# New bookings in a planner: the durations by which a hybrid encoder kernel orders its instructions, and the number of passes of its search

## The chip, the cores and the metric

The kernel runs on one core of one Trainium2 chip. TensorE (PE) does the matmuls and transposes, VectorE (DVE) and ScalarE (ACT) the elementwise work, GpSimd (POOL) a few short operations on columns, and SyncE (SP) issues nearly all DMA transfers. The metric is the device time of one execution in microseconds (us); lower is better.

## The reference, cut to what matters

Two requests of 512 tokens, width 1024, go through the same two layers in fp32: a differential-attention layer and a bidirectional retention layer. Each layer is

```
h = rms_norm(x, norm_g[i]);  q, k, v, gate = split(h @ w_in)
layer 0: p = softmax(rot(q) rot(k)^T);  o = (p[even head] - lam * p[odd head]) @ v      # 8 pairs of heads
layer 1: o = retention forward + retention backward, in chunks, with decay per head      # 8 heads
x = x + (rms_norm(o) * subln_g * silu(gate)) @ w_out
```

and a last rms_norm closes the trunk.

## The kernel before, in words

**Precision.** The matmuls take fp32r operands. Each factor is split into a rounded part (`hi_of`, a cast on ACT, L419) and the rest (`lo_of`, a subtraction on DVE, L422), and three products of the parts are summed (`PASSES`).

**Projections.** h @ w_in is done by a scheme of seven products instead of eight for blocks of two by two. The blocks of h and their sums and differences (B11, B21, T1, T2, B22, T3, T4) are made once in each layer by `make_b`: the PE transposes x into a PSUM bank (L1098), and DVE and ACT scale it by the norm's gains. A combination is one DVE instruction (`scaled`, L484: bank times gain minus another block), with further splits (L419, L422). A `Unit` is a column block of w_in; `prep` (L587, L419, L422) makes the sums of its weight blocks, and `product` the seven products P1 to P7 of a unit. A unit of kind "pair" needs 12 matmuls of 512 columns a product (`pair`, L637); a "wide" one has four steps a product of 12 matmuls of 256 columns (`wide`, L647). The sums of banks are L690 (ACT copy) and L698 (DVE), and `done` goes on from there: rotation for q and k, a silu gate (`gate_done`, L792 to L795), storing v. All of it goes out to DRAM.

**Heads.** Layer 0: scores (`scores`, L1202, 3 matmuls for each of two heads), row maxima and exponentials, a combination, a transpose (L1247), and p @ v (L1267). Layer 1: `score2` (L1400), chunk states (`state2`, L1424), products with the chunk and the far state (L1444, L1452), and norm columns (L874, L878). The output product is taken head by head (`out_step`, six matmuls of 512 columns, L950), and DVE adds it to x (L955). The last steps form the final norm and store y.

**The order.** No engine's order is written out by hand. Every operation is recorded in a list by `plan.op` with its engine, a cost in us, what it reads and writes, and, for transfers, their size. `act`, `dve`, `axpy`, `pool` and `evac` book costs that are linear in the number of elements of a partition (`dve`: 0.07 + 0.00104 n, `axpy`: 0.13 + 0.00104 n, `act`: 0.1 + 0.00083 n); `pe` gets its cost as a number. At the end, `issue` calls `arrange` several times. One call plays the whole list through on five engines (PE, ACT, DVE, POOL, SP) with the booked costs. An operation is ready once all that it depends on is done, with fixed extra times between engines (`AFTER`, `SAME`). Transfers share a bus of 380 KB a us. Whenever an engine is free it takes

- on the PE: the ready operation that is first in the program's order, at most 24 places ahead of the first one not done (`WINDOW`);
- elsewhere: the ready operation with the earliest due time (`late`). Due times are worked out backwards from the starts of the PE operations that were found in the pass before, less the costs between;
- on SP: a load only when its due time is less than 15 us away (`AHEAD`).

The first pass takes as starts the plain sum of the PE costs; each further one takes those that the pass before gave. The order of the pass with the shortest span by this count is issued. It is then fixed: each engine runs its instructions in that order and waits by semaphores. Buffers are rings (`Buf`), whose places are taken in the order of the program, and this also restricts what may be moved.

Of the kernel before, what the change touches and what calls it, by code (L numbers as in the profile page):

```python
# [16 lines left out]
S = 512  # L17
# [51 lines left out]
class Plan:  # L69
# [161 lines left out]
                    known(s)  # L231
        return out, begin, max(free.values())

    def issue(self, rounds=3):
        starts, now = {}, 0.0
        for n, op in enumerate(self.ops):
            if "PE" in op[0]:
                starts[n] = now
                now += op[0]["PE"]
        best = None  # L240
        for _ in range(rounds):
            out, begin, span = self.arrange(starts)
            if best is None or span < best[1]:
                best = (out, span, begin)
            starts = {n: begin[n] for n in starts}
        self.best = best
        for n, e in best[0]:
            costs, fn = self.ops[n][:2]
            if len(costs) > 1:
                fn(e)  # L250
            else:
                fn()
# [3 lines left out]
def trunk_kernel(  # L256
# [133 lines left out]
    def dve(n, fn, r, w, wait=0.0):  # L390
        plan.op("DVE", 0.07 + 0.00104 * n, fn, r, w, wait=wait)
# [77 lines left out]
    def make_b(layer, source):  # L469


        def parts(name, k, hi, lo, r):
            t = slot(B_SLOT[name] + k, [P, 2, S])
            hi(lambda: t[:, 0, :], r, [(t, 0)])
            lo(lambda: t[:, 1, :], lambda: t[:, 0, :], r + [(t, 0)], [(t, 1)])
            Bop[name, k] = t

        def split(name, k, src, key):
            parts(name, k, lambda out, r, w: hi_of(S, out, src, r, w),
                  lambda out, hi, r, w: lo_of(S, out, src, hi, r, w), [key])  # L480

        def scaled(out, ps, scale, less, r, w):

            dve(S, lambda: nc.vector.scalar_tensor_tensor(  # L484
                out(), ps.t, scale(), less(), op0=ALU.mult, op1=ALU.subtract), [ps, gcol] + r, w)

        def split_bank(name, k, ps, scale):
            parts(name, k, lambda out, r, w: plan.op(
                "ACT", 0.1 + 0.00092 * S,
                lambda: nc.scalar.activation(out(), ps.t, AF.Copy, scale=scale()), r + [gcol], w),  # L490
                lambda out, hi, r, w: scaled(out, ps, scale, lambda: hi().bitcast(F32), r[1:], w), [ps])

        def copy(out, ps, scale, late=()):
            evac(S, out[0], lambda: ps.t, scale, [ps, gcol, *late], [out[1]])

        def sub(out, a, b):

            dve(S, lambda: nc.vector.tensor_tensor(out[0](), a[0](), b[0](), op=ALU.subtract),
                [a[1], b[1]], [out[1]])

        def half(t, i):
            return (lambda: t[:, i, :]), (t, i)

        def whole(t):
            return (lambda: t.t), t

        two = [os_t(F32, "h") for _ in range(3)]
        h11 = [half(two[k // 2], k % 2) for k in range(4)]
        h21 = [whole(m_t("h")) for _ in range(4)]
        for name, h, k0 in (("B11", h11, 0), ("B21", h21, 4)):  # L510
            for k in range(4):
                if (name, k) in Bop and layer == 0:
                    for n in range(2):
                        ps, src = turned[n][k // 2], slice(k % 2 * 256, k % 2 * 256 + 256)
                        here = slice(n * 256, n * 256 + 256)
                        evac(256, lambda h=h[k][0], here=here: h()[:, here], lambda ps=ps, src=src: ps[:, src],
                             lambda k=k: gain(0, k), [ps, gcol, (Bop[name, k], (1, n))], [h[k][1]])
                    yield
                    continue
                bank_ = source(0, k0 + k)  # L520
                if layer == 0:
                    split_bank(name, k, *bank_)
                copy(h[k], *bank_, [(Bop[name, k], 1)] if layer == 0 else [])
                if not (layer == 0):
                    split(name, k, *h[k])
                yield
        t = [whole(e_t("h")), whole(e_t("h")), half(two[2], 0), half(two[2], 1)]
        for k in range(4):
            ps, scale = source(1, k)
            scaled(t[k][0], ps, scale, h11[k][0], [h11[k][1]], [t[k][1]])  # L530
            split("T1", k, *t[k])
            yield
        for k in range(4):
            ps, scale = source(1, 4 + k)
            scaled(t[k][0], ps, scale, t[k][0], [t[k][1]], [t[k][1]])
            split_bank("B22", k, ps, scale)
            split("T2", k, *t[k])
            sub(h11[k], t[k], h11[k])
            split("T3", k, *h11[k])
            yield  # L540
        for k in range(4):
            sub(h21[k], h21[k], t[k])
            split("T4", k, *h21[k])
            yield


    class Unit:
# [76 lines left out]
        def product(self, op, part=None):  # L624
# [27 lines left out]
            if not self.wide:  # L652
                ps = self.banks[which][0]
                if op == "P1" and self in first_units[:2]:
                    def piece(k, half):
                        here = slice(half * 256, half * 256 + 256)
                        for i, (u, v) in enumerate(PASSES):
                            nc.tensor.matmul(
                                ps[:, here], a[u][0]()[:, k, :], bt[k][:, v, here], start=(half + k + i == 0),
                                stop=(k == 3 and i == 2), skip_group_check=True)  # L660
                    if self is first_units[1]:
                        for k in range(4):
                            pe(0.7, lambda k=k: pair(ps, (k,)), reads[:2] + [bt[k]], [(ps, k)])
                        return
                    for half in range(2):
                        for k in range(4):
                            pe(0.36, lambda k=k, half=half: piece(k, half),
                               ([(a[0][1][0], (n, k // 2)) for n in range(2)] if self is first_units[0] else reads[:2])
                               + [(bt[k], (0, half)), (bt[k], (1, half))], [(ps, (k, half))])
                elif part is not None:  # L670
                    ks = range(2 * part, 2 * part + 2)
                    pe(1.4, lambda: pair(ps, ks), reads[:2] + [bt[k] for k in ks], [ps])
                else:
                    pe(2.79, lambda: pair(ps), reads, [ps])
                return
            for t in range(NT):
                ps = self.banks[which][t // 2]
                led = self.led and op == "P1" and t == 0
                pe(1.87 if led else 1.43, lambda ps=ps, t=t: wide(ps, t), reads + [ident] * led, [ps])

        def evac(self, op):
            n = 2 if self.wide else 1
# [103 lines left out]
    def gate_done(dst, gc):  # L786

        def done(i, g, tiles, s, psum):
            x = tiles[0]
            th = m_t("th") if psum else s[("c1", "c2")[g] if i == 0 else "c5"][0]  # L790
            out = th if psum else x
            act(S, lambda: nc.scalar.activation(th.t, x.t, AF.Tanh, scale=0.5), [x], [th])  # L792
            dve(S, lambda: nc.vector.scalar_tensor_tensor(out.t, th.t, 1.0, x.t, op0=ALU.add, op1=ALU.mult),
                [th, x], [out])
            act(S, lambda: nc.scalar.activation(out.t, out.t, AF.Copy, scale=gcol[:, gc + i:gc + i + 1]),  # L795
                [out, gcol], [out])
            dma(lambda: dst[g][:, i, :], lambda: out.t, [out], [(dst[g], i)], 256)
        return done
# [131 lines left out]
    def out_step(w, h, g, t, i, o, rr, last, parts=1):  # L930
# [9 lines left out]
        for p in range(parts):  # L940
# [5 lines left out]
            def fn(here=here, ps=ps):  # L946
                m = 0
                for e in range(2):
                    for a, b in PASSES:
                        nc.tensor.matmul(ps[:, here], o[a][:, e, t * P:(t + 1) * P], u[b][:, e, here],  # L950
                                         start=(m == 0), stop=(m == 5))
                        m += 1
            pe(1.39 / parts, fn, [(o[0], t // 2), (o[1], t // 2), *u], [ps])
            half = x[:, i * S + p * n:i * S + (p + 1) * n]
            axpy(n, lambda half=half, here=here, ps=ps: nc.vector.scalar_tensor_tensor(  # L955
                half, ps[:, here], rr[:, t % 2:t % 2 + 1], half, op0=ALU.mult, op1=ALU.add),
# [236 lines left out]
    def scores(i):  # L1193
        h, g, t = tiles[i]
        st[i]['s'] = []
        for j in range(2):
            s = bank("sc")
            q, k = qk[h, g, j, 0], qk[h, g, j, 1]

            def fn(s=s, q=q, k=k):  # L1200
                for n, (a, b) in enumerate(PASSES):
                    nc.tensor.matmul(s.t, q[:, a, t * P:(t + 1) * P], k[:, b, :], start=(n == 0), stop=(n == 2))  # L1202
            pe(0.7, fn, [q, k], [s])
            st[i]['s'].append(s)

    def row_max(i):
# [184 lines left out]
    def score2(b, c):  # L1391
# [5 lines left out]
        def fn():  # L1397
            for j in range(2):
                for i, (u, v) in enumerate(PASSES):
# [1 line left out]
                        s[:, j * 256:(j + 1) * 256], k[:, u, (2 * c + j) * P:(2 * c + j + 1) * P],  # L1401
                        q[:, v, c * 256:(c + 1) * 256], start=(j == 0 and i == 0), stop=(i == 2),
                        skip_group_check=True)
        pe(0.71, fn, [q, k], [s])
        t1 = e_t("rt")
        F = Fs[h]
        dve(S, lambda: nc.vector.tensor_tensor(
# [211 lines left out]
```

## Time and profile before

| | us |
|---|---|
| median of 3 runs | 1801.41 |
| lowest and highest | 1800.41, 1801.71 |
| the profiled execution | 1800.16 |
| its span, first to last instruction | 1798.3 |

The granted clock of TensorE was 0.999 of full speed. The program has 27855 instructions and moves 328.81 MB by DMA. A line in a group's row is a line of the kernel; `arena` holds the split blocks and most operands of the heads, `ws` the split weights, `raw` and `st` weights and their sums, `pj`, `sc`, `o` and `tp` are PSUM banks. In rows of the timeline, the brackets tell how long the engine was idle before the instruction and what ended it. Matmuls are pipelined: their durations overlap, and the time that one takes up is read from the spacing, as the chain of waits has it.

### The profile page before, as it was taken

The page shows a single profiled execution, that of the slowest core. Times are in us where ns is not written, and L with a number is a line of the kernel's source. Part 1 is how long each engine was busy: PE and PEld are TensorE (multiplying, and loading weights), DVE is VectorE, ACT ScalarE, POOL GpSimd, SP SyncE. Part 2 cuts the span into 40 slices and gives each one's busy share as a digit, 9 for nine tenths or more (in the row PEclk, how much of TensorE's full clock was granted, in tenths as well). Part 3 has the DMA queues.
Part 4 walks back from the last instruction along what each step waited for, and adds up shares of the span by engine and source line. Part 5 has one row for each costly group of instructions (what it writes and reads, how often), then busy time and mean ns, then how long its engine had stood idle before and what let it go on. Part 6 is the DMA issues. An engine that isn't in the chain of part 4 may idle for free.

```text
span 1798.3 us, 27855 instructions
## 1 busy us (share of the span) xinstructions
PE 1785.4 (99%) x10321; PEld 1562.1 (87%) x10321; DVE 1478.8 (82%) x2341; ACT 895.6 (50%) x1864; POOL 169.4 (9%) x315
## 2 busy tenths in 40 slices
PE   9999999999999999999999999999999999999998
PEld 7889889898988888888888888898989988888887
DVE  8967878778699888888888897777887967888887
ACT  8754344443344565455455866444434455444446
POOL 1000000000000022322232200000000000111113
PEclk9999999999999999999999999999999999999999
DMA  6444555654545695444454524465646459664652
GB/s 219 135 140 130 161 153 161 199 164 153 177 123 184 204 345 196 165 171 161 167 205 141 199 70 142 152 200 164 214 145 227 141 188 403 262 236 176 231 214 94
DMA packets 162767, 328.81 MB, mean 183 GB/s; under 512 B 12724, under 2 KB 76872, under 8 KB 162632
## 3 DMA queue, kind: packets, MB, share of 16 engines
q1 hardware_dynamic: 162304, 326.71, 53.4%
q8 instruction: 81, 1.33, 0.3%
q14 instruction: 54, 0.44, 0.1%
q10 hardware_dynamic: 328, 0.34, 0.1%
HBM read 209.55 MB, written 117.44 MB: 182 GB/s over the span
## 4 chain that ended last, share of the span: by engine, by line
PE 93%; DVE 3%; ACT 1%; DMA 1%; issue 0%; POOL 0%; SPq 0%; POOLq 0%; DVEq 0%; ACTq 0%
PE pj L637 20%; PE pj L950 19%; PE sc L637 10%; PE pj L647 10%; PE o L637 8%; PE o L1267 5%; PE sc L1202 5%; PE sc L647 5%; PE o L647 2%; PE o L1444 2%; PE tp L1247 2%; PE sc L1400 1%; PE o L1452 1%; PE tp L1424 1%; DMA raw<-in_ret_w_out_dram 1%; DVE ws L422 1%
## 5 line engine op out<-in xcount | busy, mean ns | idle before, releaser
L950 PE MATMUL pj<-ws,arena 128*128 128x512 f32 x1542 | 389.5, 396 | 0.0
L950 PEld LDWEIGHTS pj<-ws,arena 128*128 128x128 f32 x1542 | 277.5, 188 | 50.9
L637 PE MATMUL pj<-b,ws 128*128 128x512 f32 x1080 | 263.2, 390 | 0.0
L637 PEld LDWEIGHTS pj<-b,ws 128*128 128x128 f32 x1080 | 201.3, 188 | 41.3
L955 DVE SCALAR_TENSOR_TENSOR b<-pj,pad,b 128x512 f32<-128x512 f32 (+1 forms) x257 | 190.2, 744 | 23.0 <-PE pj L950 21.7
L422 DVE TENSOR_TENSOR ws<-st,ws 128x512 fp32r<-128x512 f32 (+1 forms) x192 | 148.0, 774 | 71.3 <-ACT ws L419 53.0
L422 DVE TENSOR_TENSOR ws<-raw,ws 128x512 fp32r<-128x512 f32 (+2 forms) x165 | 141.7, 863 | 68.7 <-ACT ws L419 59.1
L419 ACT CAST ws<-st 128x512 fp32r<-128x512 f32 (+1 forms) x192 | 132.2, 693 | 121.2 <-PE pj L637 36.8
L637 PE MATMUL sc<-arena,ws 128*128 128x512 f32 x768 | 185.2, 389 | 0.0
L637 PE MATMUL o<-arena,ws 128*128 128x512 f32 x744 | 178.4, 391 | 1.1 <-DVE arena L484 1.1
L637 PEld LDWEIGHTS sc<-arena,ws 128*128 128x128 f32 x768 | 143.9, 188 | 29.8
L419 ACT CAST ws<-raw 128x512 fp32r<-128x512 f32 (+2 forms) x165 | 126.0, 769 | 85.3 <-PE o L637 45.5
L637 PEld LDWEIGHTS o<-arena,ws 128*128 128x128 f32 x744 | 138.5, 188 | 30.3 <-DVE arena L484 2.0
L637 PE MATMUL pj<-arena,ws 128*128 128x512 f32 x636 | 156.1, 390 | 0.0
L637 PEld LDWEIGHTS pj<-arena,ws 128*128 128x128 f32 x636 | 118.6, 188 | 24.3
L1220 ACT ACTIVATE b<-sc,pad 128x512 f32<-128x512 f32 x128 | 87.9, 689 | 66.3 <-DVE pad L1210 64.7
L690 ACT COPY c<-pj 128x512 f32<-128x512 f32 x104 | 61.0, 587 | 116.1 <-PE pj L637 62.7
L647 PE MATMUL pj<-ws,b 128*128 128x256 f32 x960 | 116.9, 275 | 0.0
L647 PEld LDWEIGHTS pj<-ws,b 128*128 128x128 f32 x960 | 113.3, 188 | 0.6
L1202 PE MATMUL sc<-arena 128*128 128x512 f32 x384 | 100.7, 394 | 0.0
L1267 PEld LDWEIGHTS o<-arena 128*128 128x128 f32 x768 | 93.2, 188 | 2.7
L1267 PE MATMUL o<-arena 128*128 128x256 f32 x768 | 93.7, 277 | 0.0
(223 smaller groups left out, 2870.9 us busy)
## 6 DMA issues: line engine op xcount, KB each, us to landing
qk<-os SPq DMA_DIRECT2D x192, 256.0 KB, 3.5
arena<-qk SPq DMA_DIRECT2D x96, 512.0 KB, 5.7
raw<-in_da_w_in_dram SPq DMA_DIRECT2D x64, 512.0 KB, 4.9
v<-os SPq DMA_DIRECT2D x64, 512.0 KB, 3.8
arena<-v SPq DMA_DIRECT2D x64, 512.0 KB, 4.1
raw<-in_ret_w_in_dram SPq DMA_DIRECT2D x48, 512.0 KB, 4.4
os<-g SPq DMA_DIRECT2D x32, 512.0 KB, 7.8
g<-e SPq DMA_DIRECT2D x48, 256.0 KB, 4.8
```

The lines of the kernel that those rows point to most:

```text
L419: act(n, lambda: nc.scalar.copy(dst(), src()), r, w)
L422: dve(n, lambda: nc.vector.tensor_tensor(dst(), src(), hi().bitcast(F32), op=ALU.subtract), r, w)
L637: nc.tensor.matmul(ps.t, a[u][0]()[:, k, :], bt[k][:, v, :], start=(opens and k == 0 and i == 0), stop=(k == 3 and i == 2), skip_group_che ...
L647: nc.tensor.matmul(ps[:, (t % 2) * 256:(t % 2) * 256 + 256], bt[k][:, v, t * P:(t + 1) * P], a[u][0]()[:, k, :], start=(opens and t % 2 == ...
L690: act(S, lambda c=c, ps=ps: nc.scalar.copy(c.t, ps.t), [ps], [c])
L950: nc.tensor.matmul(ps[:, here], o[a][:, e, t * P:(t + 1) * P], u[b][:, e, here], start=(m == 0), stop=(m == 5))
L955: axpy(n, lambda half=half, here=here, ps=ps: nc.vector.scalar_tensor_tensor(half, ps[:, here], rr[:, t % 2:t % 2 + 1], half, op0=ALU.mult ...
L1202: nc.tensor.matmul(s.t, q[:, a, t * P:(t + 1) * P], k[:, b, :], start=(n == 0), stop=(n == 2))
L1220: act(840, lambda j=j, s=s, m=m: nc.scalar.activation(p[:, j, :], s.t, AF.Exp, bias=m.t, accum_out=sm[:, 2 * j + n:2 * j + n + 1]), [s, m] ...
L1247: nc.tensor.transpose(tp[:, j * P:(j + 1) * P], p[:, 0, j * P:(j + 1) * P], ident.t)
L1267: nc.tensor.matmul(o[:, e * 256:(e + 1) * 256], v[b][:, j, e * P:(e + 1) * P], aT[a][:, j, :], start=(n == 0), stop=(n % 12 == 11), skip_g ...
L1444: nc.tensor.matmul(o[:, e * 256:(e + 1) * 256], v_[v][:, 2 * c + j, e * P:(e + 1) * P], a_[:, u, j * 256:(j + 1) * 256], start=(e == 0 and ...
```

## The change

What changes is the number of passes (three to eight), eight booked costs of PE operations, and two bookings of elementwise work. `scaled` is recorded by `axpy` instead of `dve`, which issues the same instruction and books 0.06 us more. The last step of a gate on ACT is booked with 120 elements more. No instruction, buffer, transfer or dependence changes; only the order within each engine's queue can.

```diff
@@ -231,7 +231,7 @@
                     known(s)
         return out, begin, max(free.values())
 
-    def issue(self, rounds=3):
+    def issue(self, rounds=8):
         starts, now = {}, 0.0
         for n, op in enumerate(self.ops):
             if "PE" in op[0]:
@@ -481,7 +481,7 @@
 
         def scaled(out, ps, scale, less, r, w):
 
-            dve(S, lambda: nc.vector.scalar_tensor_tensor(
+            axpy(S, lambda: nc.vector.scalar_tensor_tensor(
                 out(), ps.t, scale(), less(), op0=ALU.mult, op1=ALU.subtract), [ps, gcol] + r, w)
 
         def split_bank(name, k, ps, scale):
@@ -660,7 +660,7 @@
                                 stop=(k == 3 and i == 2), skip_group_check=True)
                     if self is first_units[1]:
                         for k in range(4):
-                            pe(0.7, lambda k=k: pair(ps, (k,)), reads[:2] + [bt[k]], [(ps, k)])
+                            pe(0.681, lambda k=k: pair(ps, (k,)), reads[:2] + [bt[k]], [(ps, k)])
                         return
                     for half in range(2):
                         for k in range(4):
@@ -669,14 +669,14 @@
                                + [(bt[k], (0, half)), (bt[k], (1, half))], [(ps, (k, half))])
                 elif part is not None:
                     ks = range(2 * part, 2 * part + 2)
-                    pe(1.4, lambda: pair(ps, ks), reads[:2] + [bt[k] for k in ks], [ps])
+                    pe(1.362, lambda: pair(ps, ks), reads[:2] + [bt[k] for k in ks], [ps])
                 else:
-                    pe(2.79, lambda: pair(ps), reads, [ps])
+                    pe(2.725, lambda: pair(ps), reads, [ps])
                 return
             for t in range(NT):
                 ps = self.banks[which][t // 2]
                 led = self.led and op == "P1" and t == 0
-                pe(1.87 if led else 1.43, lambda ps=ps, t=t: wide(ps, t), reads + [ident] * led, [ps])
+                pe(1.81 if led else 1.367, lambda ps=ps, t=t: wide(ps, t), reads + [ident] * led, [ps])
 
         def evac(self, op):
             n = 2 if self.wide else 1
@@ -792,7 +792,7 @@
             act(S, lambda: nc.scalar.activation(th.t, x.t, AF.Tanh, scale=0.5), [x], [th])
             dve(S, lambda: nc.vector.scalar_tensor_tensor(out.t, th.t, 1.0, x.t, op0=ALU.add, op1=ALU.mult),
                 [th, x], [out])
-            act(S, lambda: nc.scalar.activation(out.t, out.t, AF.Copy, scale=gcol[:, gc + i:gc + i + 1]),
+            act(S + 120, lambda: nc.scalar.activation(out.t, out.t, AF.Copy, scale=gcol[:, gc + i:gc + i + 1]),
                 [out, gcol], [out])
             dma(lambda: dst[g][:, i, :], lambda: out.t, [out], [(dst[g], i)], 256)
         return done
@@ -950,7 +950,7 @@
                         nc.tensor.matmul(ps[:, here], o[a][:, e, t * P:(t + 1) * P], u[b][:, e, here],
                                          start=(m == 0), stop=(m == 5))
                         m += 1
-            pe(1.39 / parts, fn, [(o[0], t // 2), (o[1], t // 2), *u], [ps])
+            pe(1.366 / parts, fn, [(o[0], t // 2), (o[1], t // 2), *u], [ps])
             half = x[:, i * S + p * n:i * S + (p + 1) * n]
             axpy(n, lambda half=half, here=here, ps=ps: nc.vector.scalar_tensor_tensor(
                 half, ps[:, here], rr[:, t % 2:t % 2 + 1], half, op0=ALU.mult, op1=ALU.add),
@@ -1200,7 +1200,7 @@
             def fn(s=s, q=q, k=k):
                 for n, (a, b) in enumerate(PASSES):
                     nc.tensor.matmul(s.t, q[:, a, t * P:(t + 1) * P], k[:, b, :], start=(n == 0), stop=(n == 2))
-            pe(0.7, fn, [q, k], [s])
+            pe(0.685, fn, [q, k], [s])
             st[i]['s'].append(s)
 
     def row_max(i):
@@ -1401,7 +1401,7 @@
                         s[:, j * 256:(j + 1) * 256], k[:, u, (2 * c + j) * P:(2 * c + j + 1) * P],
                         q[:, v, c * 256:(c + 1) * 256], start=(j == 0 and i == 0), stop=(i == 2),
                         skip_group_check=True)
-        pe(0.71, fn, [q, k], [s])
+        pe(0.7, fn, [q, k], [s])
         t1 = e_t("rt")
         F = Fs[h]
         dve(S, lambda: nc.vector.tensor_tensor(
```

## The prediction

> **What bounds the kernel now.** I read the head of the page first, then the waits of the PE, then the stretches in which they fall.
>
> ```profile
> span 1798.3 us, 27855 instructions
> PE 1785.4 (99%) x10321; PEld 1562.1 (87%) x10321; DVE 1478.8 (82%) x2341; ACT 895.6 (50%) x1864; POOL 169.4 (9%) x315
> ```
>
> The PE (TensorE's matmuls) is busy for 1785.4 of 1798.3 us. A busy PE need not be at its peak, but an order can't make a matmul shorter. So an order of the same instructions can only win or lose in the remaining 12.9 us. The waits of the PE say where they lie (total, times, longest):
>
> ```profile
> PE tp L1098 <- DVE arena L484: 1.9, 2, 1.1
> PE sc L1075 <- DVE pad L431: 1.2, 1, 1.2
> PE o L637 <- DVE arena L484: 1.1, 3, 0.8
> PE tp L874 <- DVE b L422: 0.8, 1, 0.8
> PE tp L1098 <- ACT os L404: 0.5, 1, 0.5
> PE sc L1125 <- DVE b L406: 0.4, 1, 0.4
> PE sc L1125 <- DVE pad L1085: 0.3, 1, 0.3
> ...
> 1785.78 5.67 PE L950 MATMUL pj<-ws,arena 128*128 128x512 f32 x30
> ```
>
> The seven waits add up to 6.2 us. The last matmul ends at 1785.78 + 5.67 = 1791.45 us, so 6.85 us of the span come after it. Together that is the 12.9, to within the overlap of roundings. Four waits (1.2, 0.5, 0.4, 0.3) are the start of the program. The two of L484 (1.9 + 1.1 = 3.0 us) belong to `scaled`, the one line whose cost the change raises on VectorE (DVE). They fall in two places, the start of each layer:
>
> ```profile
> 23.44 8.33 PE L637 MATMUL o<-arena,ws 128*128 128x512 f32 x36
> ...
> 32.40 2.99 PE L637 MATMUL sc<-arena,ws 128*128 128x512 f32 x12
> ...
> 36.01 3.01 PE L637 MATMUL o<-arena,ws 128*128 128x512 f32 x12
> ...
> 39.66 2.98 PE L637 MATMUL sc<-arena,ws 128*128 128x512 f32 x12
> 43.73 0.66 PE L1098 MATMUL tp<-ident,b 128*128 128x128 f32 x4 [1.09 <-DVE arena L484]
> ...
> 44.99 3.02 PE L637 MATMUL o<-arena,ws 128*128 128x512 f32 x12 [0.17 <-DVE arena L484]
> 48.77 0.50 PE L637 MATMUL o<-arena,ws 128*128 128x512 f32 x1 [0.76 <-DVE arena L484]
> ```
>
> In layer 0 the PE loses 1.09 + 0.17 + 0.76 = 2.02 us; what remains of the 3.0, some 0.95 us, is layer 1. DVE is the engine that is full there (columns: PE, PEld, DVE, ACT, POOL busy in each stretch, clock, DMA share, GB/s):
>
> ```profile
> 0.00:45.00 45.00, 41.42 (x212) 33.92 (x212) 36.85 (x83) 37.24 (x71) 5.91 (x12) 1.00 0.62 218
> 45.00:90.00 45.00, 44.24 (x194) 36.31 (x195) 44.34 (x74) 32.16 (x57) 0.00 (x0) 1.00 0.42 135
> ...
> 1035.00:1080.00 45.00, 44.05 (x202) 36.17 (x201) 45.00 (x75) 30.16 (x54) 0.00 (x0) 1.00 0.24 77
> 1080.00:1125.00 45.00, 45.00 (x201) 37.24 (x200) 31.38 (x49) 27.94 (x49) 0.00 (x0) 1.00 0.40 135
> ...
> 1485.00:1530.00 45.00, 44.24 (x278) 39.30 (x277) 35.55 (x61) 22.79 (x53) 4.01 (x8) 1.00 1.03 408
> ```
>
> From 1035 to 1080 us DVE is busy for all 45.00 us; in the stretch behind it, for 31.38. The wait of 0.8 us at L874 is in the last row, where the second layer's heads begin: there DMA is full (1.03 of its time, 408 GB/s), while DVE and ACT are not.
>
> **The change, part by part.** It adds and removes no instruction and no byte. It alters durations from which an order is worked out, so its whole effect goes through the place of instructions in five queues. First I ask whether the new durations are nearer to the trace.
>
> ```profile
> 73.54 8.16 PE pj L637 x36
> ...
> 172.05 5.44 PE pj L647 x48
> ...
> 1775.04 13.64 PE pj L950 x60
> ```
>
> A pair product is 12 matmuls of L637: 8.16 / 3 = 2.72 us, booked so far at 2.79, now at 2.725. A wide step is 12 of L647: 5.44 / 4 = 1.36, booked at 1.43, now 1.367. A step of the output product is 6 of L950: 13.64 / 10 = 1.364, booked at 1.39, now 1.366. So the planner has believed in a PE that is 2 to 5 per cent too slow, and therefore in that much more time for DVE.
>
> ```profile
> 1044.48 0.74 DVE L484 SCALAR_TENSOR_TENSOR e<-tp,pad,e 128x512 f32<-128x512 f32 x1
> 1045.13 0.74 DVE L484 SCALAR_TENSOR_TENSOR e<-o,pad,e 128x512 f32<-128x512 f32 x1
> 1045.79 0.68 DVE L422 TENSOR_TENSOR ws<-st,ws 128x512 fp32r<-128x512 f32 x1
> 1046.39 0.74 DVE L484 SCALAR_TENSOR_TENSOR arena<-tp,pad,arena 128x512 fp32r<-128x512 f32 x1
> ```
>
> DVE starts the next instruction 0.65 to 0.66 us after an L484 began, and 0.60 us after an L422. The old booking of `scaled` is 0.07 + 0.00104 x 512 = 0.602 us, the new one 0.662: the new one is right. The Trainium skill, "Perfetto Trace Analysis", section "DVE / Act Engine Instruction", says that the reported window runs up to the acknowledgement of the write; so a duration may exceed the spacing, as the 0.74 beside 0.66 does. Were the 0.74 the right booking, the change would stop halfway, and the sum would be that of the rival "nothing" below; the spacing decides for 0.66.
>
> ```profile
> 1492.89 0.72 ACT L795 ACTIVATE m<-m,pad 128x512 f32<-128x512 f32 x1 [0.76 <-DVE m L793]
> 1493.52 0.60 ACT L419 CAST arena<-e 128x512 fp32r<-128x512 f32 x1
> ```
>
> L795 of ScalarE (ACT) takes up 1493.52 - 1492.89 = 0.63 us, booked at 0.525 and now at 0.625. ACT is at half load, so I cost this edit at nothing; its cover is DVE and ACT slack behind a gate, where nothing of the PE waits. If that cover were gone, the store of a gate would be 0.1 us later.
>
> Now the two starts of a layer. `scaled` runs four times for T1, four for T2 and four for B22, and in layer 0 four more for B21: 16 and 12 times. The old booking leaves out 16 x 0.06 = 0.96 us and 12 x 0.06 = 0.72 us of DVE. The rows of layer 0 above hold 36 + 4 x 12 = 84 matmuls, seven pair products, booked 7 x 0.07 = 0.49 us too long. So the planner thought DVE 1.45 us better off against the PE than it was, and there the PE lost 2.02 us: **most of this stall was not visible to the order that caused it**. In layer 1 the hidden part is 0.72 + some 0.35 (five products) = 1.07, against 0.95 us lost.
>
> What can an order that sees the stall do? It can let L484 go ahead of preparation (L422, L587) and sums (L698), each 0.60 us, or take another product forward. Against it: DVE is full, and what is put back is due soon after. For it: behind the full stretch DVE has 45.00 - 31.38 = 13.6 us free. The trace has no such order, so I bound it: all goes (-2.02 and -0.95), or each start gets two 0.60 us instructions in front of L484 by a worse choice (+1.2 each, +2.4). I take half of the gain, since a full DVE can only be given another order and not less work: -1.0 and -0.5. Both ends stay for the range.
>
> The other terms: the start of the program waits for the loads of x and a chain across four engines, and the last 6.85 us are a chain of short DVE, ACT and POOL work and a store; neither has a cost that changes beyond 0.02 us a step. I take 0 for each, from -0.6 to +0.6 (one DVE instruction of 0.60 either way). The L874 wait is set by loads: 0, its bounds are in the rival below. More changes of kind between products cost the PE a little: one more of 0.03 us for each, ten of them, +0.3. The five extra passes choose the shortest by the planner's own count; on the chip that is worth 0 by itself.
>
> Sum: -1.0 - 0.5 + 0.3 = -1.2 us. The profiled execution took 1800.16 us (span 1798.3 and 1.86 around it) and would take 1798.96. It lies 1.25 us below the median of 1801.41, so the forecast for the median is 1801.41 - 1.2 = **1800.2 us**.
>
> **The rivals.** *All stalls go*: layer starts and the L874 wait, 2.02 + 0.95 + 0.8 = 3.8 us, 1797.6 us. For it speaks that the hidden 1.45 and 1.07 us are most of what was lost; against it the 45.00 of 45.00 us and the full DMA. *Nothing*: program order, buffer turns and a full DVE leave the order as it is where it matters, or the stall moves to the next product: 1801.4 us. *A late load*, the slower one. Its place is the start of the heads of layer 1:
>
> ```profile
> 1479.85 6.67 DMA raw<-in_ret_w_out_dram
> ...
> 1489.74 9.80 DMA raw<-in_ret_w_out_dram
> ...
> 1500.89 7.94 DMA g<-e
> ```
>
> The chain of waits runs through transfers there, 24.4 us of them, although the PE idles for 0.8 us only: so there is next to no slack. SP issues nearly all transfers from one queue, in the order of the planner. A 512 KB transfer at 408 GB/s takes 1.28 us. A load that the new due times put ahead of the one that the PE needs costs that much; from the third on (3.8 us) the kernel is slower by over 0.2%. The four tiles of x of one group, put ahead, cost 5.1 us: 1806.5. Against it: only the durations of compute change, by a few per cent, and the bandwidth in the planner does not. Within it lies a case of its own: such a wait in one piece, behind which the PE goes on at half pace. One product at half pace costs another 2.7 us, 1809.2 in all; the longest waits here are 1.2 us, and the clock stays at 1.00 in the rows above, so I give it 0.02. The Trainium skill, "TensorE: Matmul & The Clock Gate", section "HAM oscillation", names idle gaps of more than some 3.4 us as what halves the clock; no run here shows one.
>
> **How the numbers follow.** Forecast 0.45; nothing 0.25; all stalls go 0.12; a late load 0.18 (with the 0.02). About 0.2%, 3.6 us, is what a measurement of this kernel can tell from no change. Forecast and nothing lie within it: same 0.70. Faster 0.12 (1797.6 is just beyond 1797.8), slower 0.18. The range goes from 1797.5, all stalls gone, to 1805.0, which is the forecast with the worse choices at both layer starts (1801.4 + 2.4 = 1803.8) and one load of 1.28 more. It leaves out the longer part of the late loads, about 0.12, and half of the fastest case, 0.06.
>
> **What would show it.** PE busy time within 1 us of 1785.4, as a proof that only gaps can change. The PE's wait for L484 at 1 to 2 us in place of 3.0; if it is 3.0 again, the step from hidden cost to order has failed; if it is near 0, I was too careful. DVE rows at 0.66 us of spacing, and at the layer starts fewer L587 and L698 directly ahead of L484. The wait at L874, or another one near 1500 us, at no more than 1 us; one above 3 us is the late load. The stretch behind the last matmul at 6.3 to 7.5 us. The forecast is wrong if gaps open where there are none now, in the long stretches where DVE runs at 82% and the PE at 100%: nothing in the trace shows the slack of each product there.

## The result, and the profile after

| | before | after |
|---|---|---|
| median of 20 runs, us | 1801.35 | 1798.27 |
| lowest and highest | 1799.94, 1802.21 | 1797.25, 1802.39 |
| the profiled execution | 1800.16 | 1797.39 |
| its span | 1798.3 | 1795.2 |
| end of the last matmul | 1791.45 | 1788.17 |

The ratio is 0.9986, with a 95% interval of 0.9980 to 0.9992: 1.4 to 3.6 us are gained, which is within the 0.2% that was called "same". (The interval leaves out 1, so these runs resolve less than the 3.6 us that the prediction took as their limit.) The profiled executions differ by 2.8 us and their spans by 3.1.

The head of the page and the waits of the PE, after (total, times, longest):

```profile
span 1795.2 us, 27855 instructions
PE 1784.5 (99%) x10321; PEld 1562.0 (87%) x10321; DVE 1482.9 (83%) x2340; ACT 897.9 (50%) x1865; POOL 156.4 (9%) x315
```

```profile
PE sc L1075 <- DVE pad L431: 1.2, 1, 1.2
PE sc L1098 <- ACT b L404: 1.0, 1, 1.0
PE pj L637 <- DVE e L698: 0.5, 1, 0.5
PE sc L1125 <- ACT b L404: 0.3, 1, 0.3
PE sc L1125 <- DVE pad L1085: 0.3, 1, 0.3
```

The count of instructions is the same, but on balance DVE has one less than before (2341) and ACT one more (1864). So more than the order has changed: an operation that is recorded by `evac` may run on DVE or on ACT, and the planner chooses the engine too.

PE busy time is down by 0.9 us only; the waits went from 6.2 to 3.3 us. No wait for L484 is left in the table, and the wait at L874 near 1509 us is gone. The places of the old and of the new waits, in the timeline of the PE:

```profile
39.42 2.99 PE L637 MATMUL sc<-arena,ws 128*128 128x512 f32 x12
42.24 0.60 PE L1098 MATMUL o<-ident,b 128*128 128x128 f32 x4
42.68 0.60 PE L1098 MATMUL tp<-ident,b 128*128 128x128 f32 x4
43.04 8.45 PE L637 MATMUL o<-arena,ws 128*128 128x512 f32 x36
51.32 1.52 PE L637 MATMUL pj<-b,ws 128*128 128x512 f32 x6
...
71.06 4.37 PE L637 MATMUL pj<-b,ws 128*128 128x512 f32 x18 [0.53 <-DVE e L698]
...
1028.88 0.33 PE L1098 MATMUL sc<-ident,b 128*128 128x128 f32 x1 [1.03 <-ACT b L404]
```

At 42 us, where the kernel before lost 2.02 us in three waits, the PE now runs without a gap: the transposes come in another order and three products follow in one stretch. Some of it comes back 22 us later: 0.53 us for a sum (L698). In layer 1 the 0.94 us of L484 are gone as well, but 1.03 us for a scaling of x (L404) have come 16 us earlier. In the kernel before that scaling was one of DVE's, and shorter:

```profile
1029.14 0.75 DVE L406 TENSOR_SCALAR b<-b,pad 128x1024 f32<-128x1024 f32 x1 [0.43 <-POOL pad L983]
```

In the changed kernel it runs on ACT and takes 1.15 us (row at run 8).

So the ledger of the listed waits is: start 1.15 to 0.61 (without the 1.17 ahead of the first matmul), layer 0 2.02 to 0.53, layer 1 0.94 to 1.03, the heads of layer 1 0.76 to 0. That is 2.7 us; the stretch behind the last matmul is 0.2 longer (6.85 to 7.03). The other 0.6 us come for the most part from what a listed wait leaves out: it begins where the matmul before it ends, although matmuls without a gap overlap (before, a product at 70.66 us lasts 2.88 us and the next begins 2.72 us after its start). The starts of the same instructions show the whole. In the kernel before, the product that begins at 39.66 us and all up to this row

```profile
54.34 1.52 PE L637 MATMUL pj<-b,ws 128*128 128x512 f32 x6
```

take 14.68 us; in the changed kernel the same 48 matmuls and 8 transposes take 51.32 - 39.42 = 11.90. The stall of layer 0 was worth 2.78 us, not 2.02.

DVE's order shows what was moved. Before, then after:

```profile
46.17 1.28 DVE L422 TENSOR_TENSOR b<-e,b 128x512 fp32r<-128x512 f32 x2
47.37 0.68 DVE L422 TENSOR_TENSOR arena<-os,arena 128x512 fp32r<-128x512 f32 x1
47.97 0.74 DVE L484 SCALAR_TENSOR_TENSOR arena<-o,pad,arena 128x512 fp32r<-128x512 f32 x1
...
70.96 0.68 DVE L698 TENSOR_TENSOR e<-pj,c 128x512 f32<-128x512 f32 x1
```

```profile
44.81 0.75 DVE L484 SCALAR_TENSOR_TENSOR arena<-o,pad,arena 128x512 fp32r<-128x512 f32 x1
...
46.69 1.28 DVE L422 TENSOR_TENSOR b<-e,b 128x512 fp32r<-128x512 f32 x2
...
70.22 0.69 DVE L698 TENSOR_TENSOR e<-pj,c 128x512 f32<-128x512 f32 x1
```

The L484 on which the last of the three waits hung now goes ahead of the three splits (L422) that stood in front of it. The sum for which the PE waits near 71 us comes only 0.74 us earlier than before, while the PE has come 54.34 - 51.32 = 3.02 us earlier: that is the 0.53.

The stretches in which the prediction read DVE, after (PE, PEld, DVE, ACT, POOL busy, clock, DMA share, GB/s):

```profile
1035.00:1080.00 45.00, 44.92 (x206) 36.93 (x205) 45.00 (x75) 31.63 (x56) 0.00 (x0) 1.00 0.27 88
...
1485.00:1530.00 45.00, 45.00 (x289) 40.57 (x289) 37.40 (x64) 23.47 (x56) 4.31 (x8) 1.00 1.04 411
```

DVE is as full as before at the layer start (45.00 of 45), and the PE is busy for 44.92 in place of 44.05 us. Nearly the same work is there (the changed kernel is some 1.3 to 2.2 us ahead); its order lets the PE go on. DMA stays full at the start of the heads, without a wait of the PE.

### The profile page after: what moved, and what is told of

Same layout as the page of the kernel before. It is cut to its first block, busy times and chain, and to the rows that moved or that the text cites. A ratio compares the mean times of both kernels' runs of the same rounds, so it can differ in the third digit from the quotient of the medians.

```text
span 1795.2 us, 27855 instructions
## 1 busy us (share of the span) xinstructions
PE 1784.5 (99%) x10321; PEld 1562.0 (87%) x10321; DVE 1482.9 (83%) x2340; ACT 897.9 (50%) x1865; POOL 156.4 (9%) x315
## 4 chain that ended last, share of the span: by engine, by line
PE 95%; DVE 3%; ACT 1%; DMA 1%; issue 0%; POOL 0%; POOLq 0%; ACTq 0%; DVEq 0%
PE pj L637 21%; PE pj L950 19%; PE sc L637 11%; PE pj L647 10%; PE o L637 8%; PE o L1267 5%; PE sc L1202 5%; PE sc L647 5%; PE o L1444 2%; PE o L647 2%; PE tp L1247 2%; PE sc L1400 1%; PE tp L1424 1%; PE o L1452 1%; DVE ws L422 1%
## 5 line engine op out<-in xcount | busy, mean ns | idle before, releaser
L955 DVE SCALAR_TENSOR_TENSOR b<-pj,pad,b 128x512 f32<-128x512 f32 (+1 forms) x257 | 190.2, 745 | 18.8 <-PE pj L950 17.9
L422 DVE TENSOR_TENSOR ws<-st,ws 128x512 fp32r<-128x512 f32 (+1 forms) x192 | 148.0, 775 | 63.2 <-ACT ws L419 56.4
L422 DVE TENSOR_TENSOR ws<-raw,ws 128x512 fp32r<-128x512 f32 (+2 forms) x165 | 142.0, 864 | 65.8 <-ACT ws L419 56.8
```

The source lines that it names most:

```text
L422: dve(n, lambda: nc.vector.tensor_tensor(dst(), src(), hi().bitcast(F32), op=ALU.subtract), r, w)
```

## The experiments

Theories: **hidden stall** (the old bookings hid the waits from the planner, above all L484's), against **passes** (the search won by being longer) and **draws** (any change gives another order, whose time scatters). All ratios are to the kernel before, on the same chip, with 95% intervals.

**1. Eight passes, old bookings.**

```diff
-    def issue(self, rounds=3):
+    def issue(self, rounds=8):
```

> The kernel before with eight passes in place of three, all bookings old. Theory (the bookings made the stall of the layer starts visible): the old bookings still hide it, so the PE waits some 3.0 us for L484 in all and the time is that of before within 0.7 us. Rival A (the extra passes did it): most of the 3 us gain, 1798.5. Rival B (any change draws another order, and its time scatters): anything within 2 us either way, with waits in new places.

Measured: 0.9997 (0.9988 to 1.0005), median 1799.99 beside 1800.70. Waits of its PE:

```profile
PE o L637 <- DVE arena L484: 1.1, 3, 0.7
PE tp L1098 <- DVE arena L484: 0.9, 2, 0.8
PE tp L874 <- DVE b L422: 0.7, 1, 0.7
```

The wait in layer 0 stays, with 1.65 us in place of 2.02. (In layer 1 the 0.94 us became 0.36: 3.0 us in all have become 2.0, so that part of the expectation missed.) The passes alone make no time that can be seen.

**2. The booking of `scaled` alone**, three passes.

```diff
-            dve(S, lambda: nc.vector.scalar_tensor_tensor(
+            axpy(S, lambda: nc.vector.scalar_tensor_tensor(
                 out(), ps.t, scale(), less(), ...
```

> The kernel before with one edit: the 28 combinations of L484 are booked 0.06 us dearer. Theory: this alone takes the 2.0 us of layer 0 away, and with it two thirds of the gain: 1799.3; the waits near 1048 us (0.9) become smaller, the one of L874 near 1509 us (0.8) stays. Rival A (passes): 1801.4, waits as before. Rival B (another draw): a time within 2 us of before, with no link to L484.

Measured: 0.9984 (0.9975 to 0.9993), median 1798.10. Waits of its PE:

```profile
PE tp L874 <- DVE b L422: 0.6, 1, 0.6
...
PE tp L1098 <- DVE arena L484: 0.4, 1, 0.4
```

All that was left of 3.0 us for L484 is 0.4, and L874's wait stays, as the theory had it. One edit of 0.06 us in a booking gives a gain that can't be told from the whole change.

**3. The bookings of the PE alone**, three passes (the eight numbers of the diff, nothing else).

> The kernel before with the eight bookings of the PE alone changed, three passes. Theory: this shortens the PE's plan by 2 to 5 per cent, but a wait for L484 stays hidden by the 0.96 us that DVE is booked short: some 1 us of the 2.0 in layer 0 stays, and the time is 1800.4. Rival A (passes): 1801.4. Rival B: within 2 us, waits in new places.

Measured: 0.9991 (0.9982 to 1.0000), median 1798.95. A row of its PE's waits, and the two waits in layer 0:

```profile
PE tp L1098 <- DVE arena L484: 1.3, 2, 0.8
```

```profile
44.34 0.66 PE L1098 MATMUL tp<-ident,b 128*128 128x128 f32 x4 [0.76 <-DVE arena L484]
...
45.59 8.45 PE L637 MATMUL o<-arena,ws 128*128 128x512 f32 x36 [0.60 <-DVE arena L484]
```

Part of the stall was hidden by the slow PE of the old bookings: 1.36 of 2.02 us remain in layer 0 when that alone is mended. The wait at L874 is gone; of the edits up to here this is the only one that takes it away. The fourth edit, the dearer last step of a gate on ACT, was not run alone; by the planner's own count, worked out from the code, it leaves the layer starts as they are.

**4. All bookings, three passes.**

```diff
-    def issue(self, rounds=8):
+    def issue(self, rounds=3):
```

> The changed kernel with three passes in place of eight. Theory: the bookings do it, so nearly all of the gain stays: 1798.3 to 1799.3, without a wait for L484 in layer 0. Rival A (passes): 1801.4. By the planner's own count the order of the third pass is 1.6 us longer than the best of eight; if that count holds on the chip to the microsecond, 1799.9, which lies between the two.

Measured: 0.9984 (0.9975 to 0.9993), median 1797.95. No wait for L484; the one of 0.53 us for L698 near 71 us is here too. So the passes from four to eight can't be seen in the time, although the planner counts 1.6 us for them. Its plan for three passes had waits of some 1.1 us near 640 us and of 0.6 near 1020; on the chip they were 0.19 us and nothing.

**5. `scaled` booked too cheap.** The kernel before, 0.542 us in place of 0.602.

```diff
-            dve(S, lambda: nc.vector.scalar_tensor_tensor(
+            dve(S - 58, lambda: nc.vector.scalar_tensor_tensor(
```

> The kernel before, with the combinations of L484 booked 0.06 us cheaper than before (0.542 us, where they take 0.66). Theory: an error of the booking goes straight into the order, so the stall of layer 0 is as long as in the kernel before or longer, 2.0 to 3 us, and the time 1800.7 to 1802. Rival B (any other set of bookings draws an order whose time scatters within 2 us): as likely better as worse than before.

Measured: 1.0005 (0.9996 to 1.0014), median 1801.48 beside 1800.40. Its timeline in layer 0:

```profile
44.31 0.66 PE L1098 MATMUL tp<-ident,b 128*128 128x128 f32 x4 [1.58 <-DVE arena L484]
...
49.35 5.74 PE L637 MATMUL o<-arena,ws 128*128 128x512 f32 x24 [1.20 <-DVE arena L484]
```

That is 2.78 us, and 4.0 over both layers. By the booking, layer 0 loses 2.78 us at 0.54, 2.02 at 0.60 and none at 0.66 (run 2): the stall follows the error, which draws would hardly do. The planner's own count for the three orders, worked out from the code, has a wait in this place of 0.58, 0.82 and 0 us. So 2.2, 1.2 and 0 us of the stall were hidden from it. The 0.82 us were not: it saw them and left them, since its rule goes by due times and does not search for the stall. The time itself can't be told from before.

**6. `scaled` booked too dear.** The changed kernel, 0.74 us in place of 0.66.

```diff
-            axpy(S, lambda: nc.vector.scalar_tensor_tensor(
+            axpy(S + 75, lambda: nc.vector.scalar_tensor_tensor(
```

> The changed kernel with L484 booked at 0.74 us, the duration that the profile reports, in place of 0.66, the spacing. Theory (spacing decides): the planner now sees DVE fuller than it is by 28 x 0.08 = 2.2 us; it moves work away from a stall that does not exist, and the time is that of the changed kernel or up to 1 us longer, 1798 to 1799. If the reported duration were what an instruction costs, this would be the better booking: 1797.5 or less. Rival B: anything within 2 us.

Measured: 0.9984 (0.9975 to 0.9993), median 1797.55. A row of its PE's waits:

```profile
PE pj L637 <- DVE e L698: 1.1, 1, 1.1
```

The wait for L698, 0.53 us in the changed kernel, is 1.13 us here: what goes too far behind L484 is missing soon after. In the time that is not to be seen, so this run doesn't decide between spacing and reported duration; with the reported duration nothing is better either.

**7. Another draw.** The changed kernel, all PE bookings dearer by a thousandth.

```diff
     def pe(cost, fn, r, w, wait=0.0):
-        plan.op("PE", cost, fn, r, w, wait=wait)
+        plan.op("PE", cost * 1.001, fn, r, w, wait=wait)
```

> The changed kernel with every booking of the PE dearer by a thousandth: no nearer to the trace and no farther, but an order of its own. Theory: the time of the changed kernel within 0.7 us, and no wait for L484 above 0.5 us. Rival B (draws scatter): the time moves by 1 to 2 us and the waits lie in other places.

Measured: 0.9984 (0.9975 to 0.9993), median 1798.06: the changed kernel's time. Its waits are others, though: 0.6 for a weight near 11 us and 0.2 for L484, and neither the 1.03 nor the 0.53. Draws shift waits of up to 1 us; they did not bring back the stall of layer 0.

**8. A dear power on POOL.** The wait for L404 that came with the change begins at POOL. Three engines of the changed kernel there:

```profile
1024.76 1.89 DVE L422 TENSOR_TENSOR arena<-m,arena 128x512 fp32r<-128x512 f32 x3
1024.81 2.84 POOL L983 TENSOR_TENSOR pad<-pad,pad 128x1 f32<-128x1 f32 x1 [2.16 <-ACT pad L976]
1026.57 0.69 DVE L587 TENSOR_TENSOR st<-st,raw 128x512 f32<-128x512 f32 x1
...
1027.68 1.15 ACT L404 ACTIVATE b<-b,pad 128x1024 f32<-128x1024 f32 x1 [1.98 <-POOL pad L983]
```

POOL's power of one element a partition takes 2.84 us; the median of the sixteen is 0.55. The edit books it at 2.79 in `finished`, which ends a row of layer 0:

```diff
-    def row_norm(g, t):
+    def row_norm(g, t, n=200):
-        pool(200, lambda: nc.gpsimd.tensor_tensor(r.t, ...
+        pool(n, lambda: nc.gpsimd.tensor_tensor(r.t, ...
-        r = row_norm(g, t)
+        r = row_norm(g, t, 1100)
```

> The changed kernel with one more booking: the power on POOL in the row norms of layer 0 (L983) at 2.79 us in place of 0.63. In the changed kernel one of them took 2.84 us, beside DVE instructions that read two operands, and the PE then waited 1.03 us for the scaling behind it. Theory (a booking that is too low hides a wait): the planner puts other products there, the wait for L404 near 1029 us falls below 0.5, and the time by 0.5 to 1 us, to 1797.5. Rival (the wait is set by DVE and ACT being full): the wait moves on to another product and the time stays at 1798.3. Rival B: within 2 us.

Measured: 0.9981 (0.9972 to 0.9989), median 1796.91. Rows of its PE's waits:

```profile
PE sc L1400 <- DMA arena<-qk: 0.6, 1, 0.6
PE pj L1098 <- DVE b L955: 0.5, 1, 0.5
```

The wait for L404 is gone, and the longest L983 takes 1.08 us. But it is gone in runs 4 and 7 too, which have the old booking of L983 (their longest take 0.97 and 0.87 us): that this booking took it away is not shown. Two others of 0.5 and 0.6 have come, one of them for a load at the heads of layer 1. The median has the sign that was expected, but its interval overlaps that of the changed kernel: not told apart.

**9. One pass.**

```diff
-    def issue(self, rounds=8):
+    def issue(self, rounds=1):
```

> The changed kernel with one pass in place of eight. By the planner's own count its order is 4.5 us longer than the best of eight, 3.2 us of them in one wait of the PE for a product at the start of layer 1, some 1 us more in the first 15 us. Theory (with bookings near the trace, a stall that the planner counts is a stall on the chip): a wait of 2 to 4 us near 1025 to 1050 us, and 1801.5 to 1803. Rival C (the count is no guide: between three and eight passes it said 1.6 us, and the two could not be told apart): 1798 to 1799.5, no such wait.

Measured: 1.0030 (1.0019 to 1.0042), median 1806.52 beside 1800.62: slower than the kernel before, and more so than either theory said. Its waits, then a stretch of 2 us and three of 6 us (columns as above):

```profile
PE sc L1098 <- ACT b L404: 3.3, 1, 3.3
...
PE tp L1098 <- ACT os L404: 1.1, 1, 1.1
PE sc L1125 <- ACT b L404: 1.0, 1, 1.0
PE pj L637 <- DVE arena L422: 1.0, 1, 1.0
PE sc L1125 <- DVE b L406: 1.0, 1, 1.0
```

```profile
15.00:17.00 2.00, 2.00 (x10) 2.00 (x11) 2.00 (x7) 1.71 (x4) 0.00 (x0) 0.50 1.05 427
...
1026.00:1032.00 6.00, 2.45 (x11) 1.81 (x11) 5.07 (x9) 3.44 (x9) 3.42 (x1) 0.99 0.90 318
1032.00:1038.00 6.00, 5.30 (x19) 4.82 (x20) 4.81 (x8) 5.28 (x10) 0.00 (x0) 0.50 0.01 5
1038.00:1044.00 6.00, 6.00 (x26) 4.88 (x25) 3.57 (x7) 2.21 (x4) 0.00 (x0) 0.94 0.00 0
```

The planned wait of 3.2 us is there in size, though it waits for something else. The column of the clock (third from the end) falls to 0.50 for some six us behind the gap, and near 15 us too, behind three waits of 1.0 to 1.1 us: the PE's matmuls run at half pace there, and its busy time is 3.9 us above that of the changed kernel. The rest are the waits. One of the six runs has a mean granted clock of 0.999 and takes 1803.76 us; the three with 0.996 and 0.997 take 1806.68 to 1807.10. Rival C falls: a plan that is bad by several us is bad on the chip. That one pass is so much worse and three are as good as eight places the worth of the passes in the second and third.

**10. All of it:** the edit of 8, PE bookings times 0.999, twenty passes.

```diff
+    def issue(self, rounds=20):
+        plan.op("PE", cost * 0.999, fn, r, w, wait=wait)
```

> The changed kernel with the dear booking of L983 in the row norms of layer 0, the bookings of the PE cheaper by a thousandth, and twenty passes, of which the shortest is taken. Theory (more draws with sound bookings win little, because only waits of 0.2 to 0.6 us are left): 1796.5 to 1797.5, no wait of the PE above 0.7 us after the first 20 us. Rival B (draws scatter): 1795.5 to 1799.

Measured: 0.9981 (0.9972 to 0.9990), median 1797.18, longest wait behind the start 0.53 us. It beats the kernel before; from the changed kernel it can't be told. What is left for an order is below what the runs resolve.

## Why the prediction was right, and where a term was mis-sized

*Only gaps can change*: right. PE busy time moved by 0.9 us.

*Most of the stall of layer 0 was hidden by the old bookings*: right, and shown by runs 2, 3 and 5, with 1.2 of 2.02 us by the planner's count (run 5) where the prediction had 1.45. The booking of `scaled` is the main part (2.02 us to none), the PE's bookings the lesser one (2.02 to 1.36).

*"I take half of the gain, since a full DVE can only be given another order and not less work: -1.0 and -0.5"*: this term was mis-sized. In layer 0 the whole 2.02 us went, and 0.53 came back: -1.5. By the starts the stall was 2.78 us, more than the bound of 2.02, which the prediction took from the listed waits. The argument itself held: DVE is as full as before, and the sum near 71 us came too late for a PE that was 3 us ahead. What was too high is the half; what came back was a quarter. The 13.6 us that the prediction set against it lie behind the start of layer 1; behind that of layer 0 its own row has DVE at 44.34 of 45. In layer 1 the L484 term went too (-0.94, all but 0.05), but a new wait of 1.03 us took its place: +0.1 in sum. It hangs on POOL and on the scaling behind it, which the new plan had given to ACT, 0.40 us slower than DVE; that the planner may change an engine is missing in the prediction.

*L874 at 0*: missed by 0.76 us. I held it to be set by loads. Run 3 takes it away with the bookings of the PE alone, runs 1 and 2 leave 0.7 and 0.6 of it; so another order of the same transfers and instructions can cure it. SP's order is another there too: a load of output weights that goes out at 1479.85 us before, behind two loads of the heads, goes out ahead of them in run 3 and in the changed kernel. Whether the place of loads or of DVE's and ACT's instructions does it was not tried.

*Start within 0.6 us*: -0.54 by the waits, inside; the product that begins at 23.44 us before begins only 0.24 us earlier. *Changes of kind, +0.3*: not told apart from the rest. *The five passes at 0*: right (runs 1 and 4).

*A late load*: it did not come with the change; a wait of 0.6 us for a load came in run 8. *Half pace behind a gap*: it came in run 9, though for POOL and ACT instead of a load. The Trainium skill, "TensorE: Matmul & The Clock Gate", section "HAM oscillation", tells of idle gaps over some 3.4 us; the trace agrees in kind at 1032 us, with 3.34 us of idle, a first gap of 1.00 us two us ahead of it, and 0.50 of the clock afterwards. It does not near 15 us, where the clock fell to 0.50 and no gap was above 1.12 us.

Sum: -1.2 forecast, -3.1 by the medians and -2.5 by the ratio. The likeliest case was too careful. That the measured time lies by the rival "all stalls go" (1797.6) is luck: a stall of 1 us had taken another's place, and the stall of layer 0 was worth more than its waits. (The upper end of the range starts from 1801.4, the kernel before, and not from the forecast as it says; the sum is 1805.1.)

## What to carry to other kernels

An order that is planned from durations leans on the bookings of the engine that is full: here an error of 0.06 us in a kind of instruction that occurs 16 times in a stage went with 2 to 3 us of stall, and five more passes of the search did not see it. A booking that is too low hides a wait; one that is too high (run 6) could not be told from the spacing in the trace. Look first at the stages where a second engine is at 100%. When the PE idles for 13 of 1800 us, read the waits first: here their sum fell by 2.9 us and the span by 3.1. Then compare the starts of the same instructions, since a wait in the list can be worth more than its length: 2.78 for 2.02 us.

## What the runs showed of the hardware that was not expected

**A short POOL instruction can be held up by a run of DVE instructions with two operands in SBUF.** In run 9, at the wait of 3.3 us:

```profile
1027.97 2.50 DVE L422 TENSOR_TENSOR arena<-m,arena 128x512 fp32r<-128x512 f32 x4
1028.05 3.42 POOL L983 TENSOR_TENSOR pad<-pad,pad 128x1 f32<-128x1 f32 x1 [4.77 <-ACT pad L976]
...
1030.38 0.69 DVE L422 TENSOR_TENSOR ws<-raw,ws 128x512 fp32r<-128x512 f32 x1
```

The run of DVE ends at 1030.38 + 0.69 = 1031.07, and POOL at 1028.05 + 3.42 = 1031.47, 0.40 us later. In the changed kernel (rows at run 8) DVE ends at 1027.26 and POOL at 1027.65, 0.39 later. In the kernel before, the same:

```profile
1024.24 1.41 DVE L955 SCALAR_TENSOR_TENSOR b<-pj,pad,b 128x512 f32<-128x512 f32 x2
1024.59 0.54 POOL L983 TENSOR_TENSOR pad<-pad,pad 128x1 f32<-128x1 f32 x1 [6.45 <-ACT pad L976]
...
1026.22 2.49 DVE L422 TENSOR_TENSOR arena<-m,arena 128x512 fp32r<-128x512 f32 x4
1027.81 1.30 POOL L983 TENSOR_TENSOR pad<-pad,pad 128x1 f32<-128x1 f32 x1 [2.68 <-ACT pad L976]
```

1028.71 and 1029.11: 0.40 again. Beside L955, which reads one operand from PSUM, the same POOL instruction takes 0.54. The Trainium skill, "GPSIMD Engine Reference", section "Key points", states that POOL shares its SBUF interfaces with VectorE and contends with instructions of two SBUF inputs; the three traces agree, and show as the price the whole remainder of the run. It need not be so. In run 3:

```profile
1023.01 1.89 DVE L422 TENSOR_TENSOR arena<-os,arena 128x512 fp32r<-128x512 f32 x3
1023.90 0.80 POOL L983 TENSOR_TENSOR pad<-pad,pad 128x1 f32<-128x1 f32 x1 [5.93 <-ACT pad L976]
```

Here POOL ends at 1024.70, before the run does (1024.90), and 0.40 us behind its second instruction, which ends at 1024.30 by the spacing of 0.60. What decides between the two is open, and no run took the DVE instructions away. The planner books POOL at a fixed 0.63 us, so such a wait is hidden from it in the way that L484's was.

**The clock fell without a long gap.** In run 9 the granted clock is 0.50 from 15 to 17 us (row at run 9). Ahead of it lie three waits, of 0.98, 1.04 and 1.12 us; from 10 to 14 us the PE is busy for 1.75 of 4 us. In the changed kernel it is busy for 3.32 us there, and the clock stays at 1.00.

**The start varies.** The first transpose with a wait near 10 us begins between 10.2 and 11.4 us in the profiles of runs 1 to 8, with nearly the same work of the PE ahead of it. No program was profiled twice, so how much of these 1.2 us is the order's can't be told. Waits are to be compared one by one, and times only over many runs.
